# First-stage tiles take the gates' first loads, the first tokens' weight splits leave GpSimd, and the base tiles' transfers move to SyncE's queue

## The chip, the cores and the metric

The kernel runs on one core of a Trainium2 chip. The metric is the device time of one execution in microseconds (us), lower is better. Engines are named as the profile names them: PE (TensorE), DVE (VectorE), ACT (ScalarE), POOL (GpSimd) and SP (SyncE, which here only issues transfers). POOL and ACT can issue transfers too; each engine works through its own instructions in program order, so a transfer that waits holds what stands behind it on that engine.

## The reference, cut to what matters

One encoder layer over 2048 tokens and 16 learned meta tokens, D = 1024, all in float32:

```python
h = layer_norm(concat([meta, x]), ln_in_g, ln_in_b)
q, k, v, u, g_attn, g_ssm = split(h @ w_in[l], SPLITS)
q = rope(rms_norm(q, q_norm_g)); k = rope(rms_norm(k, k_norm_g))
y_attn = block_attention(q, k, v)
y_ssm  = s5_branch(u, ...)                  # forward and backward scan, GELU-GLU
merged = sigmoid(g_attn) * (y_attn @ w_attn_br) + sigmoid(g_ssm) * (y_ssm @ w_ssm_br)
h = layer_norm(ALPHA * h + merged @ w_o, ln1_g, ln1_b)
moe = expert_choice_moe(h[real tokens])     # 16 experts, each takes its top 256 tokens, SwiGLU
h = layer_norm(ALPHA * h + moe, ln2_g, ln2_b)
return h[real tokens]
```

## The kernel before, in words

Products that must keep float32 are made of a high and a low part: ACT casts a weight `wr` to `wh`, DVE (or POOL) subtracts to get `wl`, and PE adds three products (high by high, high by low, low by high). Every engine's order is the order of the Python code.

**First stage** (`phase_a`). Seventeen token tiles of 128 tokens (the last holds the 16 meta tokens) are normalised (`ln_ops`, `norm`), turned by PE (`trans`: PE writes `pT`, ACT casts `hth`, DVE subtracts `htl`), and multiplied with the q/k/v columns (`qkv`, the first weights, split by `split_w(0, k)`) and the u columns (`u_mm`, the second weights, `split_w(1, k)`, which run three raw tiles deep). `rope` finishes q and k of a tile on DVE with the products `gc` and `gs` that POOL makes in `rope_prep`. `qk_trans` turns q and k with PE, casts to `qh` on ACT, subtracts to `ql` on DVE, and stores them to `q_d` and `k_d`: through SP's queue, for the last three tiles through POOL's. Each `qh` buffer is used again two tiles later, after its store has landed. A loop over s runs the stages of five neighbouring tiles side by side.

**Gates** (`gates`). A generator, started at step s = 17 of that loop, loads raw weights (512 KB each), splits them to `gwh` and `gwl`, loads the normalised, turned inputs back from `ht_d` (256 KB for each of k = 0..7 and of high and low, for four token blocks b), multiplies (`pg`, line 1230), and takes the sigmoid on ACT (`gg`, line 1201). The state-space part's first loads on ACT (lines 708 and 710) stand ahead of the first `gg`.

**Attention, merge, routing** follow and are not touched.

**Experts** (`experts`). Each of the 16 experts has 12 weights of 1 MB. An expert is 16 steps: 8 gate/up steps of 48 matmuls (gate block i and up block i are both used in steps 2i and 2i+1), then 8 down steps of 24. `ahead` in a step loads the weight three further on through SP's queue and splits the one two further on (ACT `wh`, DVE `wl`); three raw buffers let SP run ahead of the steps. The output rows are added into `acc_d` by indirect transfers of POOL, two halves per expert (`scatter`; the second half is issued in step 1 of the next expert). From expert 9 on `step` also advances side generators once per step. `finish` takes the base tiles: all 16 tiles of 128 rows of `acc_d` are read (`fx`), normalised in pairs (`norm`, ACT sums into `fj`, DVE the rest, one new pair every 11 steps) and stored to the output. `redo` does the rows that experts 9 to 14 changed again (`fa`), and the last expert normalises its own rows (`ye`) half by half. `fx` loads and stores go through POOL's queue, as `scatter`, the gathers `xg` and the indirect stores (`put_rows`) do:

```python
            def load(t):
                xs[t] = fp.tile([128, D], F32, name="fx", bufs=4)
                PL.dma_start(xs[t], acc_d[128 * t:128 * t + 128])
```

Of the kernel before, what the change touches and what calls it, by code (L numbers as in the profile page):

```python
# [10 lines left out]
F32 = mybir.dt.float32  # L11
# [33 lines left out]
def f(t):  # L45
    return t.bitcast(F32)
# [3 lines left out]
def kernel(ctx, tc, x, meta, ln_in_g, ln_in_b, w_in, q_norm_g, k_norm_g,  # L50
# [63 lines left out]
        for _ in ln_ops(*args):  # L114
            pass

    def phase_a(start_gates):
        cr = ExitStack()
        with ExitStack() as c:
            wq = cr.enter_context(pool(name="a_q", bufs=1, side="right"))  # L120
            xp = cr.enter_context(pool(name="a_x", bufs=4, side="right"))
            px = cr.enter_context(pool(name="a_px", bufs=1, space=PSUM, side="right"))
            wp = c.enter_context(pool(name="a_w", bufs=1))
            sm = c.enter_context(pool(name="a_sm", bufs=3))
# [11 lines left out]
                SP.dma_start(RC[t][0], rope_c[128 * t:128 * t + 128])  # L136
                SP.dma_start(RC[t][1], rope_s[128 * t:128 * t + 128])

            gb = wq.tile([128, D], F32, name="gb")
            bb = wq.tile([128, D], F32, name="bb")  # L140
            cols = ((0, 768), (768, 1280))
            WH, WL, WR = [], [], []
            for p, (c0, c1) in zip((wq, wp), cols):
# [18 lines left out]

            def rope_prep(t):
                cs, sn = RC[t]
                gc, gs = (xp.tile([128, 10, 64], F32, name="gc", bufs=2), xp.tile([128, 10, 64], F32, name="gs", bufs=2))
                PL.tensor_tensor(gc, g10, cs[:, None, :].to_broadcast([128, 10, 64]), op=OP.mult)
                PL.tensor_tensor(gs, s10, sn[:, None, :].to_broadcast([128, 10, 64]), op=OP.mult)
                RC[t] = gc, gs
# [123 lines left out]
            with pool(name="a_st", bufs=8) as st:  # L292
                for k in range(8):
                    load_w(st, 0, k)
                load(2)
                for _ in zip(*(ln_ops(sm, X[t], 128, gb, bb, "a") for t in range(2))):
                    pass
                for k in range(3):
                    split_w(0, k, PL)
                trans(0)  # L300
                trans(1)
                qkv(0, 0, 2)
                qkv(1, 0, 2)
                for k in range(2, 8):
                    if k > 2:
                        split_w(0, k, V)
                    qkv(0, k, k + 1)
                    qkv(1, k, k + 1)
# [12 lines left out]
                load_w(wr, 1, k)  # L321
            load(3)
            norm(2)
            for k in range(8):
                split_w(1, k, (V, PL)[k % 2])
                if k + 3 < 8:
                    load_w(wr, 1, k + 3)
                if k == 4:
                    load_rope(2)
                    load_rope(3)  # L330
# [4 lines left out]
            for s in range(NT + 4):  # L335
                if s + 4 <= NT:
                    load(s + 4)
                    if s + 4 < NT:
                        load_rope(s + 4)
                if s < NT:  # L340
                    rope_prep(s)
                if 1 <= s < NT:
                    trans(s + 1)
                if 0 <= s - 3 < NT:
                    qk_trans(s - 3, 0)
                next(gg, None)
                if 1 < s <= NT:
                    qkv(s, 0, 3)
                next(gg, None)
                if 0 <= s - 3 <= NT:  # L350
                    qk_trans(s - 3, 1)
                next(gg, None)
                if 2 < s + 2 <= NT:
                    norm(s + 2)
                if 0 <= s - 1 <= NT:
                    rope(s - 1)
                if 1 < s <= NT:
                    qkv(s, 3, 8)
                if 1 <= s <= NT:
                    u_mm((s - 1) // 2, (s - 1) % 2)  # L360
                if s == NT:
                    cr.close()
                    gg = start_gates()
                    next(gg)
                    u_meta()
        return gg
# [792 lines left out]

        yield from pipe((item(b) for b in range(4)), every=7)  # L1160

    def gates(c):
        hp = c.enter_context(pool(name="g_h", bufs=32, side="right"))
        wp = c.enter_context(pool(name="g_w", bufs=2, side="right"))
        pg = c.enter_context(pool(name="g_p", bufs=2, space=PSUM, side="right"))
        W, HB = {}, {}
        order = [(i, b) for i in range(2, 16) for b in range(2)]
        order += [(16, 2), (17, 2), (16, 3), (17, 3)] + [(i, b) for i in range(18, 32) for b in (2, 3)]
        steps = [[(0, 0), (1, 0)], [(0, 1), (1, 1)]] + [[x] for x in order]
        first = {}  # L1170
        for s, group in enumerate(steps):
            for i, b in group:
                first.setdefault(i, s)
        split_at = {first[i] if i != 17 else first[i] + 2: i + 1 for i in range(2, 31)}
        load_at = {first[i]: i + 2 for i in range(2, 30)}

        def load_w(i):
            c0 = 1280 + 128 * (i % 16)
            wr = wp.tile([128, 8, 128], F32, name="gwr")
            SP.dma_start(wr, w_in[0, :, c0:c0 + 128].rearrange("(k p) c -> p k c", p=128))  # L1180
            W[i] = wr

        def split_w(i):
            wr = W[i]
            wh = wp.tile([128, 8, 128], F32R, name="gwh")
            wl = wp.tile([128, 8, 128], F32R, name="gwl")
            A.copy(wh, wr)
            V.tensor_tensor(wl, wr, f(wh), op=OP.subtract)
            W[i] = wh, wl

        def load_h(b, k):
            r = []
            for i in range(2):
                t = hp.tile([128, 512], F32R, name="gh")
                SP.dma_start(f(t), ht_d[i, k, :, 512 * b:512 * b + 512])
                r.append(t)
            HB[b, k] = r

        def evac(i, b, p):
            g = wp.tile([128, 512], F32, name="gg")  # L1200
            A.activation(g, p, AF.Sigmoid)  # L1201
            A.dma_start(gt_d[i % 16, :, 512 * b:512 * b + 512], g)

        load_w(0)
        load_w(1)
        for k in range(8):
            load_h(0, k)
        yield
        split_w(0)
        split_w(1)  # L1210
        load_w(2)
        load_w(3)
        for k in range(8):
            load_h(1, k)
        ev = []
        for step, group in enumerate(steps):
            while len(ev) + len(group) > 2:
                evac(*ev.pop(0))
            if step in split_at:
                split_w(split_at[step])  # L1220
            if step in load_at:
                load_w(load_at[step])
            P = [pg.tile([128, 512], F32, name="pg") for _ in group]
            n = 0
            for k in range(8):
                for (i, b), p in zip(group, P):
                    wh, wl = W[i]
                    hi, lo = HB[b, k]
                    for j, (w, h) in enumerate(((wh, hi), (wh, lo), (wl, hi))):
                        PE.matmul(p, w[:, k], h, start=(k == 0 and j == 0), stop=(k == 7 and j == 2))  # L1230
                        n += 1
                        if n % 4 == 0:
                            if n == 12 and ev:
                                evac(*ev.pop(0))
                            yield
                if group[0][0] == 15:
                    load_h(b + 2, k)
            ev = [(i, b, p) for (i, b), p in zip(group, P)]
            if step == 1:
                split_w(2)  # L1240
        for e in ev:
            evac(*e)
# [428 lines left out]
    def experts(c, pos, inf):  # L1671
# [221 lines left out]
        def finish():  # L1893
            SP.dma_start(gb, row_bcast(ln2_g, D))
            SP.dma_start(bb, row_bcast(ln2_b, D))
            xs = {}

            def load(t):
                xs[t] = fp.tile([128, D], F32, name="fx", bufs=4)
                PL.dma_start(xs[t], acc_d[128 * t:128 * t + 128])  # L1900

            yield
            for t in range(2):
                load(t)
            yield
            yield

            def base(t):
                for n, _ in enumerate(norm([xs[t], xs[t + 1]])):
                    if n == 7 and t + 2 < NT:  # L1910
                        load(t + 2)
                        load(t + 3)
                    yield
                for i in range(2):
                    PL.dma_start(outs[t + i], xs.pop(t + i))

            yield from pipe((base(t) for t in range(0, NT, 2)), every=MO[3])

# [12 lines left out]
        def step(e, s):  # L1931
# [4 lines left out]
            if (e, s) == (E - 1, 1):  # L1936
                acc_rows(e)
                sides.append(redo(e - 1, MO[2]))
            for g in sides:
                next(g, None)  # L1940

        one_hot(0, 0, NT)
        pi = pick(0)
# [79 lines left out]
                pass  # L2023
        return
    cg = ExitStack()
    gg = phase_a(lambda: gates(cg))
    if stop <= 1:
        return
    with cg:
# [101 lines left out]
```

## Time and profile before

| | |
|---|---|
| three timed runs | 3157.53, 3164.89, 3165.57 us (median 3164.89) |
| the profiled execution's own time | 3158.51 us |
| its span in the trace | 3156.7 us |
| PE busy | 2978.7 us (94% of the span) |
| DVE, ACT, POOL busy | 2145.9, 1572.0, 1010.9 us |
| mean granted clock of PE | 0.977 of full speed |

The span is from the first to the last recorded instruction. All times of the trace below are counted from its start. A share of busy time is an average over stages that have different limits, so a stage is read from its own rows.

### The profile page before, as it was taken

Reading aid. Unit: us, or ns where it says so; the run is one execution under the profiler, and the core shown is the slowest. Engines: PE = TensorE matmul, PEld = TensorE weight load, DVE = VectorE, ACT = ScalarE, POOL = GpSimd, SP = SyncE. Lnnn points to the kernel's source line nnn. Section 1 sums busy time; section 2 is a strip of 40 time slices with the busy share of each in tenths; the row PEclk is TensorE's granted clock in tenths of the full one; section 3 lists DMA queues with packets and bytes.
Section 4 is the critical chain, followed back from the end, with each engine's and each line's share of the span. In section 5 each row is a group of like instructions: output and inputs, shape, how many; then the busy total and the mean of one; then the engine's idle time right before and its main releaser. Section 6 shows DMA issues by size and latency. Waiting matters only on the chain.

```text
span 3156.7 us, 56179 instructions
## 1 busy us (share of the span) xinstructions
PE 2978.7 (94%) x22829; PEld 2632.0 (83%) x22829; DVE 2145.9 (68%) x3725; ACT 1572.0 (50%) x2229; POOL 1010.9 (32%) x633
## 2 busy tenths in 40 slices
PE   6999999999989999999899996799999999999997
PEld 5887787777867777777678885699999999999997
DVE  7886589783366666666466666666666665778886
ACT  2222352243369999999622222344444444666553
POOL 3221035051069999999510001111111101122221
PEclk9999999999999999999999998799999999999999
DMA  6566633557510101013366743366677667778884
GB/s 224 186 206 186 160 104 108 185 148 203 175 45 22 35 21 35 21 35 90 110 206 199 200 134 108 134 214 206 214 220 225 217 214 230 258 260 267 274 263 157
DMA packets 464499, 513.00 MB, mean 163 GB/s; under 512 B 47568, under 2 KB 387728, under 8 KB 463856
## 3 DMA queue, kind: packets, MB, share of 16 engines
q1 hardware_dynamic: 433616, 421.20, 42.7%
q0 software_dynamic: 19232, 69.53, 7.3%
q10 hardware_dynamic: 11392, 18.68, 1.7%
q8 instruction: 179, 2.93, 0.4%
q14 instruction: 80, 0.66, 0.1%
HBM read 385.59 MB, written 123.76 MB: 161 GB/s over the span
## 4 chain that ended last, share of the span: by engine, by line
PE 62%; DVE 14%; ACT 8%; DMA 6%; issue 6%; POOL 3%; SPq 1%; ACTq 0%; POOLq 0%; DVEq 0%
PE pg L1784 18%; PE pd L1812 8%; PE pg L1230 7%; PE pw L1383 5%; PE pb L1315 5%; PE pm L449 3%; PE pS L483 3%; ACT pe L490 2%; PE pS L484 2%; PE po L520 2%; DVE wl L1692 2%; PE pz L1147 1%; ACT wh L1691 1%; POOL pl L506 1%; ACT ph L502 1%
## 5 line engine op out<-in xcount | busy, mean ns | idle before, releaser
L1784 PE MATMUL pg<-xh,wh 128*128 128x256 f32 x2048 | 573.0, 280 | 5.5 <-DVE sg L1792 4.6
L1784 PE MATMUL pg<-xh,wl 128*128 128x256 f32 x2048 | 570.3, 278 | 2.8 <-DVE wl L1692 2.8
L1692 DVE TENSOR_TENSOR wl<-wr,wh 128x2048 fp32r<-128x2048 f32 x189 | 433.2, 2292 | 204.2 <-ACT wh L1691 204.1
L1784 PE MATMUL pg<-xl,wh 128*128 128x256 f32 x2048 | 570.6, 279 | 0.0
L506 POOL TENSOR_TENSOR pl<-pe,ph 128x1024 f16<-128x1024 f32 x256 | 542.5, 2148 | 60.5 <-DVE ph L500 48.8
L455 DVE TENSOR_REDUCE mx<-pm 128x1 f32<-128x412 f32 (+1 forms) x640 | 368.6, 586 | 190.1 <-PE pm L449 174.1
L1784 PEld LDWEIGHTS pg<-xh,wh 128*128 128x128 f32 x2048 | 386.6, 189 | 6.3 <-DVE sg L1792 4.8
L1784 PEld LDWEIGHTS pg<-xh,wl 128*128 128x128 f32 x2048 | 385.8, 188 | 3.5 <-DVE wl L1692 3.4
L1784 PEld LDWEIGHTS pg<-xl,wh 128*128 128x128 f32 x2048 | 386.3, 189 | 0.0
L1691 ACT CAST wh<-wr 128x2048 fp32r<-128x2048 f32 x189 | 359.8, 1904 | 16.3 <-DMA wr<-in_w_up_e_dram 9.2
L1230 PE MATMUL pg<-gh,gwh 128*128 128x512 f32 x1024 | 337.0, 405 | 19.5 <-ACT gg L1201 14.1
L490 ACT ACTIVATE pe<-pS,ebias 128x1024 f32<-128x1024 f32 x256 | 284.8, 1112 | 37.9 <-PE pS L484 37.9
L1812 PE MATMUL pd<-wh,hh 128*128 128x256 f32 x1024 | 285.8, 279 | 7.0 <-ACT ye L1831 4.6
L1812 PE MATMUL pd<-wh,hl 128*128 128x256 f32 x1024 | 283.7, 277 | 1.5 <-DVE hl L1799 1.4
L1812 PE MATMUL pd<-wl,hh 128*128 128x256 f32 x1024 | 283.1, 276 | 0.0
L1230 PEld LDWEIGHTS pg<-gh,gwh 128*128 128x128 f32 x1024 | 195.4, 194 | 62.7 <-ACT gg L1201 16.8
L502 ACT CAST ph<-pe 128x1024 f16<-128x1024 f32 x224 | 234.4, 1046 | 16.1 <-ACT pe L490 0.4
L449 PE MATMUL pm<-k,q 128*128 128x412 f32 (+1 forms) x640 | 233.5, 375 | 9.1 <-DVE mx L455 3.1
L483 PE MATMUL pS<-q,k 128*128 128x512 f32 (+1 forms) x544 | 231.8, 426 | 10.6 <-ACT pe L490 9.2
L520 PEld LDWEIGHTS <-ph 128*128 128x128 f16 (+1 forms) x2176 | 188.7, 96 | 63.6 <-issue 60.3
L520 PE MATMUL po<-v,ph 128*128 128x129 f16 (+1 forms) x2176 | 231.5, 221 | 0.8 <-ACT t L528 0.8
L522 PE MATMUL po<-v,pl 128*128 128x65 f16 (+1 forms) x2176 | 220.2, 192 | 2.2 <-POOL pl L506 2.1
(424 smaller groups left out, 6761.5 us busy)
## 6 DMA issues: line engine op xcount, KB each, us to landing
wr<-in_w_gate_e_dram SPq DMA_DIRECT2D x64, 1024.0 KB
wr<-in_w_up_e_dram SPq DMA_DIRECT2D x64, 1024.0 KB
wr<-in_w_down_e_dram SPq DMA_DIRECT2D x64, 1024.0 KB
gwr<-in_w_in_dram SPq DMA_DIRECT2D x32, 512.0 KB
gh<-ht_d SPq DMA_DIRECT2D x64, 256.0 KB
gt_d<-gg ACTq DMA_DIRECT2D x64, 256.0 KB
gt<-gt_d SPq DMA_DIRECT2D x32, 512.0 KB
q<-q_d SPq DMA_DIRECT2D x96, 128.0 KB
```

Source lines behind the costliest of these rows:

```text
L449: PE.matmul(p[:, :w], Q[n][0][:, 128 * j:128 * j + 128], K1[units[n][1] // 4][:, k0:k0 + w], start=True, stop=True)
L455: V.tensor_reduce(MX[n][:, j, c:c + 1], p[:, :w], axis=AX.X, op=OP.max)
L483: PE.matmul(p[:m, a], K2[g][:, k0:k0 + m], Q[n][1], start=True, stop=False)
L490: A.activation(e[:m, :w], p[:m, :w], AF.Exp, bias=ebias[:m], scale=HD ** -0.5)
L502: A.copy(hi[:m, :w], e[:m, :w])
L506: (PL if w == 2 else V).tensor_tensor(lo[:m, :w], e[:m, :w], hi[:m, :w], op=OP.subtract)
L520: PE.matmul(o[:, 0:129], hi[:m, a, 128 * j:128 * j + 128], v16[:m, kt, g, 0:129], start=(kt == 0 and j % 2 == 0), stop=False, skip_group_c ...
L1230: PE.matmul(p, w[:, k], h, start=(k == 0 and j == 0), stop=(k == 7 and j == 2))
L1691: A.copy(wh, wr)
L1692: V.tensor_tensor(wl, wr, f(wh), op=OP.subtract)
L1784: PE.matmul(p[:, gu], w[:, k, cs_], x[:, k], start=(k == 0 and j == 0), stop=(k == 7 and j == 2))
L1812: PE.matmul(p, a[:, k, cs_], w[:, k], start=(k == 0 and j == 0), stop=(k == 7 and j == 2))
```

## The change

There are four edits. (1) In `phase_a` the first three weight splits of the q/k/v columns run on DVE between the turns of the first two tiles, no longer on POOL; and the normalisation of tile 3 runs two operations at a time between the splits of the second weights instead of after them. (2) The pool of the first stage's token tiles stays open. The gates' raw weights go into the two tiles that held the layer norm's gain and bias (`bb`, `gb`), and the inputs k = 0..3 of token blocks 0 and 2 into the four token tiles `x`, so that those ten loads don't wait for the stage's other pools to close; they are issued at s = 17 ahead of the stores of tile 14. The two first gate splits stand ahead of the meta tokens' u. (3) The base tiles' loads and stores go through SP's queue, and their normalisation begins four steps after the first load instead of two. (4) In the last expert from step 10 on the side generators advance twice a step.

```diff
+        xp = cg.enter_context(pool(name="a_x", bufs=4, side="right"))
...
-                for k in range(3):
-                    split_w(0, k, PL)
+                split_w(0, 0, V)
                 trans(0)
+                split_w(0, 1, V)
                 trans(1)
+                split_w(0, 2, V)
...
+            ln3 = ln_ops(sm, X[3], 128, gb, bb, "a")
             for k in range(8):
                 split_w(1, k, (V, PL)[k % 2])
+                if k > 1:
+                    next(ln3, None)
+                    next(ln3, None)
...
+                if s == NT:
+                    gg = start_gates(xp)
+                    next(gg)
                 if 0 <= s - 3 < NT:
                     qk_trans(s - 3, 0)
...
-                if 2 < s + 2 <= NT:
+                if 3 < s + 2 <= NT:
                     norm(s + 2)
...
+        def load_x(b, k):
+            t = xp.tile([128, 2, 512], F32R, name="x")
+            for i in range(2):
+                SP.dma_start(f(t[:, i]), ht_d[i, k, :, 512 * b:512 * b + 512])
+            HB[b, k] = [t[:, 0], t[:, 1]]
...
+        load_w(0)
+        load_w(1)
+        for k in range(NX):
+            load_x(0, k)
+        yield
+        hp = c.enter_context(pool(name="g_h", bufs=32 - 2 * NX, side="right"))
...
-                PL.dma_start(xs[t], acc_d[128 * t:128 * t + 128])
+                SP.dma_start(xs[t], acc_d[128 * t:128 * t + 128])
...
-            yield
-            yield
+            for _ in range(4):
+                yield
...
-                    PL.dma_start(outs[t + i], xs.pop(t + i))
+                    SP.dma_start(outs[t + i], xs.pop(t + i))
...
-            for g in sides:
-                next(g, None)
+            for _ in range(2 if (e, s) >= (E - 1, 10) else 1):
+                for g in sides:
+                    next(g, None)
```

How the instructions stand on the engines at three places. First DVE at the start, from the first two tiles' last normalising operation (L107 x2) to the splits of the first weights; line numbers of the changed kernel are one higher here. Before:

```order
L106 SCALAR_TENSOR_TENSOR x<-x,amv,gb 128x1024 x2
L107 SCALAR_TENSOR_TENSOR x<-x,ar,bb 128x1024 x2
L184 TENSOR_TENSOR htl<-pT,hth 128x4x128 x4
L157 TENSOR_TENSOR wl<-wr,wh 128x768 x5
L103 BN_STATS ast<-x 128x6 x2
```

and of the change:

```order
L106 SCALAR_TENSOR_TENSOR x<-x,amv,gb 128x1024 x2
L107 SCALAR_TENSOR_TENSOR x<-x,ar,bb 128x1024 x2
L158 TENSOR_TENSOR wl<-wr,wh 128x768
L185 TENSOR_TENSOR htl<-pT,hth 128x4x128 x2
L158 TENSOR_TENSOR wl<-wr,wh 128x768
L185 TENSOR_TENSOR htl<-pT,hth 128x4x128 x2
L158 TENSOR_TENSOR wl<-wr,wh 128x768 x6
L103 BN_STATS ast<-x 128x6 x2
```

DVE has eight splits instead of five; POOL's first tensor operations are now the second weights' (L158, 128x512), behind two copies that wait for the q and k gains.

Second, SP's queue at the end of the first stage, from the last u store of the main loop (`u_d`) over the stores of tile 14 (`q_d`, `k_d`, `v_d`) to the gates' loads. Before:

```order
L273 DMA u_d<-us 8x16x128 x4
L256 DMA q_d<-qh 128x4x128
L256 DMA q_d<-ql 128x4x128
L258 DMA k_d<-qh 128x128
L258 DMA k_d<-ql 128x128
L213 DMA v_d<-vt 128x128
L1180 DMA gwr<-in_w_in_dram 128x8x128 x2
L1195 DMA gh<-ht_d 128x512 x16
L1180 DMA gwr<-in_w_in_dram 128x8x128 x2
```

and of the change:

```order
L274 DMA u_d<-us 8x16x128 x4
L1188 DMA bb<-in_w_in_dram 128x8x128
L1188 DMA gb<-in_w_in_dram 128x8x128
L1180 DMA x<-ht_d 128x512 x8
L257 DMA q_d<-qh 128x4x128
L257 DMA q_d<-ql 128x4x128
L259 DMA k_d<-qh 128x128
L259 DMA k_d<-ql 128x128
L214 DMA v_d<-vt 128x128
L1224 DMA gh<-ht_d 128x512 x8
L1188 DMA bb<-in_w_in_dram 128x8x128
```

Ten loads (3 MB) have moved ahead of the five stores, and eight loads are left behind them.

Third, SP's queue in expert 9, from the loads of `finish`'s gain and bias (`gb_`, `bb_`) on; `wr` are the experts' weights in order, the gate block behind `bb_` is expert 9's weight 4. Before:

```order
L1895 DMA bb_22041<-in_ln_b_dram 128x1024
L1684 DMA wr<-in_w_gate_e_dram 128x8x256
L1684 DMA wr<-in_w_up_e_dram 128x8x256
L1684 DMA wr<-in_w_gate_e_dram 128x8x256
L1684 DMA wr<-in_w_up_e_dram 128x8x256
L1684 DMA wr<-in_w_down_e_dram 128x8x256 x4
```

and of the change:

```order
L1922 DMA bb_22037<-in_ln_b_dram 128x1024
L1711 DMA wr<-in_w_gate_e_dram 128x8x256
L1927 DMA fx<-acc_d 128x1024 x2
L1711 DMA wr<-in_w_up_e_dram 128x8x256
L1711 DMA wr<-in_w_gate_e_dram 128x8x256
L1711 DMA wr<-in_w_up_e_dram 128x8x256
L1711 DMA wr<-in_w_down_e_dram 128x8x256 x4
L1711 DMA wr<-in_w_gate_e_dram 128x8x256
L1711 DMA wr<-in_w_up_e_dram 128x8x256
L1927 DMA fx<-acc_d 128x1024 x2
L1711 DMA wr<-in_w_gate_e_dram 128x8x256
L1942 DMA out_dram<-fx 128x1024 x2
```

The first two `fx` loads stand between weights 4 and 5. The eight pairs of loads fall into steps 1 and 12 of expert 9, 7 of 10, 2 and 13 of 11, 8 of 12, 3 and 14 of 13; the eight pairs of stores into steps 14 of expert 9, 9 of 10, 4 and 15 of 11, 10 of 12, 5 of 13, 0 and 11 of 14.

## Rows read from the trace of the kernel before

**Rows 1.** The page's chain of work that ended last, shares by engine.

```profile
PE 62%; DVE 14%; ACT 8%; DMA 6%; issue 6%; POOL 3%; SPq 1%; ACTq 0%; POOLq 0%; DVEq 0%
```

**Rows 2.** Windows, experts 8, 9, 15: length, busy (PE, PEld, DVE, ACT, POOL), clock, DMA.

```profile
2561.92:2630.10 68.18, 68.18 (x627) 68.14 (x625) 43.46 (x64) 32.94 (x40) 7.79 (x5) 1.00 0.73 225
2630.10:2706.23 76.13, 71.50 (x626) 71.07 (x625) 49.97 (x83) 39.48 (x52) 9.43 (x11) 0.96 0.74 241
...
3069.26:3137.73 68.47, 66.20 (x578) 65.64 (x576) 48.99 (x76) 30.43 (x38) 14.61 (x9) 1.00 0.61 193
```

**Rows 3.** Timeline of DVE, start: start, length, what, [idle before <-releaser].

```profile
12.15 5.57 DVE L107 SCALAR_TENSOR_TENSOR x<-x,ar,bb 128x1024 f32<-128x1024 f32 x2
...
53.65 1.28 DVE L107 SCALAR_TENSOR_TENSOR x<-x,ar,bb 128x1024 f32<-128x1024 f32 x1
```

**Rows 4.** Timeline of POOL, the same stretch.

```profile
11.37 8.03 POOL L157 TENSOR_TENSOR wl<-wr,wh 128x768 fp32r<-128x768 f32 x3 [10.92 <-ACT wh L156]
...
45.94 1.56 POOL L166 TENSOR_TENSOR gc<-g,cs 128x640 f32<-128x640 f32 x1
```

**Rows 5.** Timeline of PE, 54 to 60 us.

```profile
55.09 1.94 PE L176 MATMUL pT<-idf,x 128*128 128x128 f32 x8 [4.30 <-DVE x L107]
58.75 0.77 PE L203 MATMUL pq<-wh,hth 128*128 128x512 f32 x1 [1.73 <-DVE sq L232]
```

**Rows 6.** Timeline of SP's queue, start of the gates.

```profile
286.91 0.40 SPq L256 DMA_DIRECT2D q_d<-qh  x1
...
290.90 13.93 SPq L1195 DMA_DIRECT2D gh<-ht_d  x16
```

**Rows 7.** Timeline of ACT, start of the gates.

```profile
300.28 0.57 ACT L251 CAST qh<-pk 128x512 fp32r<-128x512 f32 x1
...
309.42 0.59 ACT L251 CAST qh<-pk 128x512 fp32r<-128x512 f32 x1 [1.89 <-DMA q_d<-qh]
...
317.21 0.17 ACT L251 CAST qh<-pk 128x16 fp32r<-128x16 f32 x1 [4.29 <-DMA q_d<-qh]
...
319.91 1.81 ACTq L708 DMA_DIRECT2D s<-in_ssm_a_im_dram  x2
322.73 0.37 ACTq L710 DMA_DIRECT2D s<-in_ssm_log_dt_dram  x1
...
324.42 0.60 ACT L1201 ACTIVATE gg<-pg 128x512 f32<-128x512 f32 x1
```

**Rows 8.** Timeline of PE, 324 to 326 us.

```profile
325.07 1.22 PE L1230 MATMUL pg<-gh,gwh 128*128 128x512 f32 x2 [6.49 <-ACT gg L1201]
```

**Rows 9.** Timeline of SP's queue: expert 9's weight 5, expert 13's weight 7.

```profile
2634.93 0.38 SPq L1684 DMA_DIRECT2D wr<-in_w_up_e_dram  x1
...
2944.16 0.37 SPq L1684 DMA_DIRECT2D wr<-in_w_up_e_dram  x1
```

**Rows 10.** Timeline of POOL, experts 9 and 13.

```profile
2642.71 1.62 POOL L1834 DMA_INDIRECT acc_d<-ye,ix  x1 [0.30 <-ACT sg L1790]
2652.59 2.23 POOL L1900 DMA_DIRECT2D fx<-acc_d  x4 [8.26 <-DMA acc_d<-ye,ix]
...
2954.64 1.16 POOL L1900 DMA_DIRECT2D fx<-acc_d  x2 [9.01 <-DMA acc_d<-ye,ix]
```

**Rows 11.** Timeline of ACT, experts 9 and 13.

```profile
2659.00 1.06 ACT L1874 ACTIVATE fj<-fx 128x1024 f32<-128x1024 f32 x1 [8.93 <-DMA fx<-acc_d]
...
2955.05 1.92 ACT L1691 CAST wh<-wr 128x2048 fp32r<-128x2048 f32 x1 [0.39 <-DMA wr<-in_w_up_e_dram]
```

**Rows 12.** Timeline of DVE, the last expert's second half of rows.

```profile
3140.55 0.48 DVE L1818 SCALAR_TENSOR_TENSOR ye<-pd,gv,ye 128x256 f32<-128x256 f32 x1
...
3144.31 1.28 DVE L1827 SCALAR_TENSOR_TENSOR ye<-ye,lr,bb 128x1024 f32<-128x1024 f32 x1
```

**Rows 13.** Timeline of POOL, the last two stores.

```profile
3144.50 1.91 POOL L1890 DMA_INDIRECT out_dram<-ye,io  x1 [2.62 <-DMA out_dram<-fa,io]
3149.54 0.95 POOL L1890 DMA_INDIRECT out_dram<-ye,io  x1 [3.12 <-DMA out_dram<-ye,io]
```

More of the change, by code (lines that the diff above doesn't have):

```diff
@@ L115, in layer_norm, with phase_a @@
             pass
-    def phase_a(start_gates):
+    def phase_a(cg, start_gates):
         cr = ExitStack()
+        xp = cg.enter_context(pool(name="a_x", bufs=4, side="right"))
         with ExitStack() as c:
             wq = cr.enter_context(pool(name="a_q", bufs=1, side="right"))
-            xp = cr.enter_context(pool(name="a_x", bufs=4, side="right"))
+            xg = cr.enter_context(pool(name="a_g", bufs=2, side="right"))
             px = cr.enter_context(pool(name="a_px", bufs=1, space=PSUM, side="right"))
@@ L137, in load_rope @@
                 SP.dma_start(RC[t][1], rope_s[128 * t:128 * t + 128])
-            gb = wq.tile([128, D], F32, name="gb")
-            bb = wq.tile([128, D], F32, name="bb")
+            gb = xp.tile([128, D], F32, name="gb", bufs=1)
+            bb = xp.tile([128, D], F32, name="bb", bufs=1)
             cols = ((0, 768), (768, 1280))
@@ L164, in rope_prep @@
                 cs, sn = RC[t]
-                gc, gs = (xp.tile([128, 10, 64], F32, name="gc", bufs=2), xp.tile([128, 10, 64], F32, name="gs", bufs=2))
+                gc, gs = (xg.tile([128, 10, 64], F32, name="gc"), xg.tile([128, 10, 64], F32, name="gs"))
                 PL.tensor_tensor(gc, g10, cs[:, None, :].to_broadcast([128, 10, 64]), op=OP.mult)
@@ L343, in phase_a @@
                     trans(s + 1)
+                if s == NT:
+                    gg = start_gates(xp)
+                    next(gg)
                 if 0 <= s - 3 < NT:
                     qk_trans(s - 3, 0)
-                next(gg, None)
+                if s > NT:
+                    next(gg, None)
                 if 1 < s <= NT:
                     qkv(s, 0, 3)
-                next(gg, None)
+                if s > NT:
+                    next(gg, None)
                 if 0 <= s - 3 <= NT:
                     qk_trans(s - 3, 1)
-                next(gg, None)
-                if 2 < s + 2 <= NT:
+                if s > NT:
+                    next(gg, None)
+                if 3 < s + 2 <= NT:
                     norm(s + 2)
@@ L362, in phase_a @@
                     cr.close()
-                    gg = start_gates()
                     next(gg)
@@ L1160, in glu, with gates, load_w @@
         yield from pipe((item(b) for b in range(4)), every=7)
-    def gates(c):
-        hp = c.enter_context(pool(name="g_h", bufs=32, side="right"))
+    def gates(c, xp):
+        HB = {}
+        NX = 4
+        def load_x(b, k):
[3 more added lines that the diff above has]
+            HB[b, k] = [t[:, 0], t[:, 1]]
+        W = {}
+        def load_w(i):
+            c0 = 1280 + 128 * (i % 16)
+            wr = xp.tile([128, 8, 128], F32, name="gb" if i % 2 else "bb", bufs=1)
+            SP.dma_start(wr, w_in[0, :, c0:c0 + 128].rearrange("(k p) c -> p k c", p=128))
+            W[i] = wr
+        load_w(0)
[4 more added lines that the diff above has]
+        hp = c.enter_context(pool(name="g_h", bufs=32 - 2 * NX, side="right"))
         wp = c.enter_context(pool(name="g_w", bufs=2, side="right"))
         pg = c.enter_context(pool(name="g_p", bufs=2, space=PSUM, side="right"))
-        W, HB = {}, {}
         order = [(i, b) for i in range(2, 16) for b in range(2)]
@@ L1175, in gates @@
         load_at = {first[i]: i + 2 for i in range(2, 30)}
[L1177 to L1181, printed above, removed]
         def split_w(i):
@@ L1191, in load_h @@
         def load_h(b, k):
+            if b % 2 == 0 and k < NX:
+                load_x(b, k)
+                return
             r = []
@@ L1202, in evac @@
             A.dma_start(gt_d[i % 16, :, 512 * b:512 * b + 512], g)
-        load_w(0)
-        load_w(1)
-        for k in range(8):
+        for k in range(NX, 8):
             load_h(0, k)
-        yield
         split_w(0)
         split_w(1)
+        yield
         load_w(2)
@@ L1904, in finish @@
                 load(t)
-            yield
-            yield
+            for _ in range(4):
+                yield
             def base(t):
@@ L2025 @@
     cg = ExitStack()
-    gg = phase_a(lambda: gates(cg))
+    gg = phase_a(cg, lambda xp: gates(cg, xp))
     if stop <= 1:
```

## The prediction

> **What bounds the kernel now.** I read the chain of waits first: 62% of it is PE, 14% DVE, 8% ACT, 6% transfers [rows 1]. PE is the limit nearly everywhere, so the change can win only where PE stands still or where the end of the program hangs on another engine. I then cut the expert stage into windows by the first matmul of each expert. Expert 8, which has no side work, takes 68.18 us with PE busy throughout; expert 9 takes 76.13 with PE idle for 4.63 and the clock at 0.96; from expert 9's start at 2630.10 to the last matmul's end at 3137.73 pass 507.6 us, 30.4 more than seven times 68.18 [rows 2]. That is all that edits (3) and (4) could win ahead of the last matmul. Last I read the timelines of each engine at the four places that the diff touches: the start, the start of the gates, experts 9 to 13, and the tail behind 3137.73.
>
> **Edit 1, the first tokens.** POOL's three splits run from 11.37 to 19.40, and beside them DVE's two L107 take 5.57 us, where one takes 1.28 alone [rows 3, 4]. Without POOL the two take some 2.6; the first tile is ready about 1.5 us earlier, the second 3. DVE gets three splits more, of at most 2.7 us each (POOL's price, 8.03 for three [rows 4]), in gaps in which it waits for ACT's cast of the turned tile; PE's first products hide them. Tile 3's normalisation no longer stands between the last split and `rope` on DVE. In the trace PE waits 4.30 us for it at 55.09, and 1.73 at 58.75 for the `rope` work queued behind it [rows 5]. Together 6.0 us, and behind this place PE is the bound until the gates, so they would stay won. Against it: POOL's first tensor operation is now the second weights' split. Before the old first one POOL stood still for 10.92 us from the span's start [rows 4]; whatever it costs to make a tensor operation ready lay hidden in there, so it is between nothing and 10.9. The nearest row is `gc`, also a kind of work that POOL had not done before, which took 1.56 us at once [rows 4]. At nothing the edit wins 6; at 10.9 POOL's `gc` at 45.94 moves behind 55, and nothing is won. I take 5, because a few us of delay fit before tile 3's products are due.
>
> The Trainium skill bears on that cost: its page "GPSIMD Engine Reference", section "Instruction dispatch", says that the first call of a freshly loaded kernel pays some 6 us that no row of a profile shows. No row here can show it; by that figure, an estimate, the edit would win about 4 instead of 5.
>
> **Edit 2, the gates' start.** SP issues the `q_d` store of tile 14 at 286.91 and 16 input loads in 13.93 us, 0.87 each [rows 6]. Ten loads ahead of the store push it by 8.7 us to 295.6. The next `qh` cast, now at 300.28, uses that store's buffer again. Stores of this stretch land late: `qh` cast at 300.28 (0.57 us) is stored by POOL, and the cast that needs its buffer starts at 309.42, 8.6 us later [rows 7]. With 8.6 the moved store lands at 304.2 and the cast is 4 us late; with half of that it is not late. What follows hangs on it: two rounds of cast and store (300.28, 309.42, 317.21), the state-space loads to 322.73, and `gg` at 324.42 [rows 7], for which PE waits 6.49 us at 325.07 [rows 8]. So the gates' first product may well start earlier, since its data are there sooner, but it only lengthens that wait. For the change speaks that the issue at L710 starts 1.0 us after the one before it is done (319.91 and 1.81 against 322.73 [rows 7]), and that 3 MB less stand in the queues when POOL's two stores pass. I take 0 (from -4, half of both rounds' excess, to +4).
>
> **Edit 3, the base tiles on SP's queue.** This is the largest term. The first pair of `fx` must wait until expert 8's second half has been added into `acc_d`: POOL issues that at 2642.71, and the `fx` behind it goes out at 2652.59, when it has landed [rows 10]. On POOL only POOL waited. On SP the weights wait: weight 5 of expert 9 went out at 2634.93 [rows 9], and now goes out behind two `fx` (0.56 each, a quarter of 2.23) at 2653.7. How long it takes to land lies between 6.4 (the first `fx`, 2652.59 to 2659.00 [rows 10, 11]) and 10.9 (a weight of expert 13, 2944.16 to 2955.05 [rows 9, 11]); with four transfers at once I take 8: 2661.7. Cast on ACT takes 1.9 [rows 11], DVE's half about the same: 2665.5. PE wants weight 5 in the middle of step 4; a step of 48 matmuls is a twelfth of 68.18, 5.68 us, so at 2630.10 + 4.5 x 5.68 = 2655.7. PE stands for 9.8 us. The stall of before goes: ACT waited 8.93 us for `fx` at 2659.00 [rows 11] and PE 4.63; two steps more of lead put this sum behind the landing. Net +5. In expert 13 the pair in step 3 waits in the same way, until 2954.64 [rows 10]; weight 7, issued at 2944.16 [rows 9], goes out at 2955.8 and is there at 2963.8 instead of 2955.05. A weight is cast in the step for which 8.5 us are left (1.5 steps), 3.8 of them needed for the split, so 4.7 of the 8.8 are hidden, less what ACT and DVE lose: +5 with the clock that a stall costs (0.96 in expert 9 [rows 2]). Expert 11's pair, in step 2, holds weight 6, which is cast two steps ahead (7.6 hidden): +3. The eight pairs of stores hold SP until DVE has done a tile in the same step, while SP otherwise runs some two steps ahead; two down steps are 5.7 us, 4.7 of which are hidden: up to 1 each, I take 3 in all. POOL is freed of 32 transfers and their waits, so its scatters and gathers go out when they can: -4 (bounds 0 and, by the 8.93 alone, -9). Sum +12. The ends: if weights come in time after all, expert 9's 8 us vanish and ACT's waits too, -13; if each of the three late weights takes 10.9 instead of 8 and POOL's relief is nothing, +25.
>
> **Edit 4, the tail.** PE ends at 3137.73 [rows 2], but DVE takes up the last quarter of the second half's rows only at 3140.55, behind the redone rows, and ends the normalisation at 3145.59 [rows 12], 5.04 us later. POOL issues the store of the first half at 3144.50, after the redone rows' store has landed, and the second at 3149.54, when the first has landed, 5.04 later [rows 13]. With the side work done earlier DVE starts at 3137.8 and ends at 3142.9; the first half's store goes out at about 3137.8 and is landed by 3142.9 too. The last store then goes out 6.6 earlier. I take -6 (at least -2.8, DVE's part alone).
>
> **Sum.** -5 + 0 + 12 - 6 = +1, on the profiled execution's own 3158.51 (the span of 3156.7 and 1.8 around it): 3159.5. The median of the timed runs is 6.4 above the profiled execution, one of the three runs 1 below it; I add half of 6.4: **3163 us**. A difference under 0.3%, 9.5 us, can hardly be told from no change here.
>
> **The rivals.** *Weights in time (faster).* SP runs far enough ahead, or the transfers land sooner from SP's queue than from POOL's, and edit 3 only takes expert 9's stall away: -5 to -13 for it, sum about -19, 3143. For it: 30.4 us of excess in experts 9 to 15, which POOL's late `fx` began [rows 2, 11]; against it, the order in which weight 5 stands behind a transfer that cannot go before 2652. Beside it stands a rule of the Trainium skill, "SBUF — State Buffer", the warning on the "DVE blocks DMA" trap: transfers issued by GpSimd can wait for their descriptors while DVE holds the shared port, those of SP's queue don't. By it the `fx` on SP would land sooner than 6.4. No row separates the two.
>
> *SP's queue held (slower).* The pairs of `fx` and stores in SP's order delay weights by more than the lead at each of experts 9, 11 and 13: +25 for edit 3, sum +14, 3176. It decides from a landing time of about 10 us behind `fx`; expert 13's 10.9 speaks for it, the 6.4 against.
>
> *POOL's first operation is dear (no change).* Edit 1 wins nothing: sum +6, 3168.
>
> **Chances.** My forecast, with the third rival beside it, has 0.41 (within 0.3%); weights in time and a full win at the start and the tail 0.35 (faster); SP held 0.24 (slower). The range 3145 to 3179 takes in most of both sides; the forecast's own is 3154 to 3172.
>
> **What would show it.** Right: in PE's timeline no wait for L107 near 55 and the first long `pq` block some 5 us earlier; `gg` within 3 us of the same distance from the first stage's end; PE standing still in the middle of expert 9's step 4, waiting for DVE's `wl`, with weight 5 issued just after the scatter's landing; expert 13's weight 7 likewise; the span's end 12 to 13 us behind PE's end instead of 19 (3156.7 against 3137.73). Wrong: expert 9 as short as expert 8, POOL's first split later than 40, or ACT's `qh` cast past 304.

## The result and the profile after

The changed kernel takes 3194.35 us (median of 4 runs, 3189.82 to 3196.71), before 3163.55: a ratio of 1.0099, 95% interval 1.0081 to 1.0117. It is 31 us slower, where I had forecast no change (3163, range 3145 to 3179). The profiled execution took 3196.71, with a span of 3194.9, 38.2 more than before; that is more than 31 because it is the slowest of the four, and the one profiled before was among the faster.

Where the 38.2 us came in is read from where the same matmul stands in both traces. The last `pu` matmul of the first stage ends at 296.78 instead of 299.76 (-3.0). At the first matmul of expert 9, 2630.41 against 2630.10 [rows 2], nothing of this is left (+0.3; in the twelve later profiles this point lay between 2623.7 and 2630.7, also for edits that don't touch the stages between, so a few us there can't be assigned). Experts 9 to 15 take 553.8 us instead of 507.6 (+46.2). From PE's last matmul to the span's end pass 10.7 us instead of 19.0 (-8.3). The windows of the changed kernel, cut as in [rows 2] (expert 9, 12, 15, and the stretch behind PE's end):

```profile
2630.41:2709.03 78.62, 71.60 (x627) 71.08 (x625) 49.03 (x81) 37.49 (x48) 7.80 (x5) 0.93 0.68 214
...
2862.28:2950.25 87.97, 73.95 (x627) 72.64 (x625) 61.51 (x107) 43.69 (x60) 13.65 (x8) 0.92 0.70 227
...
3111.43:3184.20 72.77, 68.79 (x578) 67.73 (x576) 54.06 (x79) 31.35 (x40) 15.81 (x10) 1.00 0.64 208
...
3184.20:3194.90 10.70, 0.00 (x0) 0.00 (x0) 4.96 (x13) 0.29 (x1) 1.90 (x2) 0.64 0.25 98
```

Before, expert 12 and experts 9 to 15 together were:

```profile
2850.99:2925.91 74.92, 70.47 (x626) 69.83 (x625) 62.02 (x109) 45.05 (x62) 17.12 (x13) 1.00 0.80 266
2630.10:3137.73 507.63, 488.69 (x4322) 483.30 (x4320) 389.75 (x683) 286.72 (x382) 104.44 (x83) 0.99 0.78 253
```

Every one of the seven experts is longer, by 2.5, 2.0, 6.5, 13.0, 11.3, 6.6 and 4.3 us; expert 12 most, 88.0 instead of 74.9. Busy times of DVE and ACT over the seven have hardly changed (392.0 and 286.2 us), and the DMA share of expert 12 has fallen from 0.80 to 0.70. So it is waiting, not work. What SP's queue waited for between 2636 and 3195 us (view of waits: engine and what it wanted to issue, what released it, us in total, times, longest), the largest lines on `fx`:

```profile
SPq L1927 <- DMA acc_d<-ye,ix: 48.5, 6, 14.1
SPq L1942 <- DMA out_dram<-fa,io: 43.3, 2, 25.2
...
SPq L1942 <- DVE fx L1914: 32.1, 4, 10.0
SPq L1942 <- DVE sg L1818: 27.6, 3, 9.7
```

L1927 are the `fx` loads, L1942 the stores. The longest single wait of these, 25.2 us, is a store that waits for an indirect store of redone rows (`fa`) into the same output to land. In SP's timeline of that stretch it stands between two weights of expert 12:

```profile
2852.07 0.38 SPq L1711 DMA_DIRECT2D wr<-in_w_gate_e_dram  x1
2877.75 1.16 SPq L1942 DMA_DIRECT2D out_dram<-fx  x2
2879.00 1.69 SPq L1711 DMA_DIRECT2D wr<-in_w_up_e_dram  x1
```

POOL issues that indirect store only at 2869.76, after 60.48 us in which it waited for DVE; ACT and PE pay, in their timelines:

```profile
2869.76 5.56 POOL L1917 DMA_INDIRECT out_dram<-fa,io  x1 [60.48 <-DVE oh L1750]
```

```profile
2887.88 1.90 ACT L1718 CAST wh<-wr 128x2048 fp32r<-128x2048 f32 x1 [17.84 <-DMA wr<-in_w_up_e_dram]
```

```profile
2889.83 0.58 PE L1811 MATMUL pg<-xh,wh 128*128 128x256 f32 x1 [10.16 <-ACT wh L1718]
```

The store waits, the weight behind it goes out 27 us after the one ahead of it, ACT waits 17.84 us for that weight, PE 10.16 us for ACT. The `fx` loads do the same in expert 11: SP stands from 2790.32 until 2806.83, when a scatter has landed, ACT waits 11.78 us for the weight behind, and PE waits for work that ACT and DVE had to leave standing:

```profile
2806.83 0.81 SPq L1927 DMA_DIRECT2D fx<-acc_d  x2
2808.04 0.38 SPq L1711 DMA_DIRECT2D wr<-in_w_gate_e_dram  x1
```

```profile
2817.70 1.90 ACT L1718 CAST wh<-wr 128x2048 fp32r<-128x2048 f32 x1 [11.78 <-DMA wr<-in_w_gate_e_dram]
```

```profile
2824.39 0.55 PE L1811 MATMUL pg<-xh,wh 128*128 128x256 f32 x1 [7.64 <-DVE sg L1819]
```

The three other stages, each with a row of the changed kernel: PE at the start (beside [rows 5]), POOL's first tensor operation (beside [rows 4]), the first gate on ACT (beside [rows 7]), and the last store (beside [rows 13]):

```profile
56.08 0.47 PE L204 MATMUL pq<-wh,hth 128*128 128x512 f32 x1 [3.51 <-DVE sq L233]
```

```profile
32.53 1.29 POOL L158 TENSOR_TENSOR wl<-wr,wh 128x512 fp32r<-128x512 f32 x1 [1.48 <-ACT wh L157]
```

```profile
308.70 0.58 ACT L252 CAST qh<-pk 128x512 fp32r<-128x512 f32 x1 [5.88 <-DMA q_d<-qh]
...
322.52 0.60 ACT L1230 ACTIVATE gg<-pg 128x512 f32<-128x512 f32 x1
```

```profile
3189.93 0.95 POOL L1917 DMA_INDIRECT out_dram<-ye,io  x1 [4.53 <-DVE ye L1854]
```

### The profile page after: what moved, and what is told of

Same layout as the page of the kernel before. It is cut to its first block, busy times and chain, and to the rows that moved or that the text cites. A ratio compares the mean times of both kernels' runs of the same rounds, so it can differ in the third digit from the quotient of the medians.

```text
span 3194.9 us, 56196 instructions
## 1 busy us (share of the span) xinstructions
PE 2992.8 (94%) x22829; PEld 2644.5 (83%) x22829; DVE 2146.2 (67%) x3728; ACT 1571.1 (49%) x2229; POOL 986.1 (31%) x598
## 4 chain that ended last, share of the span: by engine, by line
PE 57%; DVE 14%; DMA 9%; ACT 8%; issue 7%; POOL 3%; SPq 1%; ACTq 0%; POOLq 0%; DVEq 0%
PE pg L1811 17%; PE pd L1839 7%; PE pg L1257 6%; PE pw L1410 5%; PE pb L1342 5%; PE pm L460 3%; PE pS L494 3%; ACT pe L501 2%; PE pS L495 2%; PE po L531 2%; PE pz L1158 1%; DVE wl L1719 1%; DMA wr<-in_w_up_e_dram 1%; ACT wh L1718 1%; POOL pl L517 1%
## 5 line engine op out<-in xcount | busy, mean ns | idle before, releaser
L1811 PE MATMUL pg<-xh,wh 128*128 128x256 f32 x2048 | 579.4, 283 | 32.6 <-ACT wh L1718 18.0
L1257 PE MATMUL pg<-gh,gwh 128*128 128x512 f32 x768 | 252.5, 405 | 8.6 <-DMA gh<-ht_d 5.6
L1861 POOL DMA_INDIRECT acc_d<-ye,ix x30 | 65.4, 2181 | 528.1 <-ACT ye L1858 517.0
```

What stands on the lines that cost most here:

```text
L1811: PE.matmul(p[:, gu], w[:, k, cs_], x[:, k], start=(k == 0 and j == 0), stop=(k == 7 and j == 2))
```

## The experiments

Theory M: SP's queue is held. A transfer that waits on SP stops all that stands behind it, and what stands behind it are the weights. Rival R: it is the bytes; 16 MB more in the weights' queue make every weight land later, whenever they are issued. Rival Q: the side work of DVE and ACT has moved (four steps, double steps) and the queue has nothing to do with it. All times are medians; the ratio is to the kernel before, timed on the same chip. "Experts" below is the length of experts 9 to 15 in the profile. One profile shows one execution: two later kernels that leave the expert stage as it was before (`only_1` and `only_2`) take 511.4 and 515.4 us there instead of 507.6, so a difference of up to 8 us between two profiles need not be an effect of the edit.

**Stores back on POOL, loads on SP** (`stores_pool`).

```diff
-                    SP.dma_start(outs[t + i], xs.pop(t + i))
+                    PL.dma_start(outs[t + i], xs.pop(t + i))
```

> The changed kernel with the base tiles' 16 stores back on POOL's queue; the 16 fx loads stay on SP's. Theory M (SP is held: each store waits on SP for DVE's last operation on its tile, and for the landing of an earlier indirect store into the output, and the weights stand behind it): the stores' share of the loss, about 28 of the 46 us in experts 9 to 15, goes; expert 12, now 88.0 us, falls below 78; time about 3166. Rival R (it is the transfers themselves: 16 MB more in the weights' queue make every weight land later, whenever they are issued): half of the transfers are gone, so about half of the loss, 3171 to 3175, and it goes evenly from all experts. Rival Q (the loss is from side work that moved on DVE and ACT, four yields and the double steps): 3190 to 3195.

3183.64 us, ratio 1.0051 (1.0035 to 1.0068); experts 542.1:

```profile
2628.10:3170.20 542.10, 499.77 (x4322) 493.73 (x4320) 392.71 (x685) 285.86 (x382) 98.42 (x68) 0.96 0.74 238
```

Q's range is missed, and so are the other two. M's number was too good by 18 us: the loads alone cost far more than I had thought, and expert 12 still takes 83.0, not under 78 (it takes 79.2 even with nothing on SP, in the run after the next).

**Loads back on POOL, stores on SP** (`loads_pool`).

```diff
-                SP.dma_start(xs[t], acc_d[128 * t:128 * t + 128])
+                PL.dma_start(xs[t], acc_d[128 * t:128 * t + 128])
```

> The changed kernel with the base tiles' 16 fx loads back on POOL's queue; the stores stay on SP's. Theory M: the weights no longer wait for scatters to land; experts 9, 11 and 13 lose their late weight 5, 6 and 7 (stalls of 7.0, 7.6 and 4.0 us in PE), expert 12 keeps its 10 us stall; about 12 to 16 us faster than the changed kernel, about 3180. Rival R: half of the loss, 3171 to 3175, from all experts alike. Rival Q: 3190 to 3195.

3179.58 us, ratio 1.0044 (1.0028 to 1.0061), as M had it; experts 536.7. Expert 9 takes 68.2 instead of 78.6, expert 12 keeps 86.8 with a wait of 10.85 us on PE. Expert 13 falls by 4.3, about as M had it, but expert 11 only by 1.9, not by 7.6.

**Both back on POOL** (`both_pool`): both diffs above.

> The changed kernel with loads and stores of the base tiles on POOL's queue, four steps between first load and first normalisation, the double steps and the rest kept. Theories M and R: the whole loss goes, experts 9 to 14 take 430 to 440 us together as before (439) or less, since expert 9's stall for the first fx goes too; the span still ends about 11 us behind PE's end instead of 19; about 3150 to 3157, faster than the kernel before. Rival Q: 3190 to 3195.

3149.03 us, ratio 0.9945 (0.9929 to 0.9962): 45 us below the changed kernel (49 by the ratios) and faster than the kernel before. Q falls: the four steps and the double steps are still in. What is won over the kernel before does not lie in experts 9 to 15 (509.8 instead of 507.6) but in the stretch behind PE's end (12.9 instead of 19.0) and ahead of expert 9 (4.9, which is within the scatter at that point). The windows for expert 9, expert 12 and experts 9 to 15:

```profile
2625.19:2693.37 68.18, 68.18 (x626) 68.14 (x625) 49.21 (x81) 37.33 (x48) 8.82 (x9) 1.00 0.82 262
2834.44:2913.59 79.15, 73.25 (x627) 72.04 (x625) 63.48 (x109) 46.33 (x64) 17.98 (x14) 0.98 0.78 258
2625.19:3134.96 509.77, 490.24 (x4322) 485.52 (x4320) 393.28 (x685) 285.50 (x382) 112.12 (x85) 0.99 0.78 253
```

Against these 509.8 the loads on SP alone cost 32.3, the stores alone 26.9, both together 44.0. The two don't add up; I take it that a weight that is late already isn't late twice, which no run tests by itself.

**Stores four steps later, on SP** (`stores_later`).

```diff
+                for _ in range(4):
+                    yield
                 for i in range(2):
                     SP.dma_start(outs[t + i], xs.pop(t + i))
```

> The changed kernel with the stores of each pair of base tiles four steps later in the program, still on SP's queue, with the same bytes. Theory M: DVE is done with the tile when SP comes to the store, so the waits on SP for DVE's operations (some 90 us in all, of which part is hidden) go; where an earlier indirect store has to land first the wait stays if that store is issued late; 15 to 28 us faster than the changed kernel, 3166 to 3179. Rival R: the transfers are the same, so 3190 to 3197. Rival Q: the same, 3190 to 3197.

3190.93 us, ratio 1.0077 (1.0060 to 1.0094): within R's range, outside M's. The waits for DVE are gone from SP's largest waits, but those for indirect stores to land are four instead of two, 34.2 us, the longest 18.0. That one has moved into expert 15, which takes 85.2 (at a granted clock of 0.90):

```profile
SPq L1927 <- DMA acc_d<-ye,ix: 51.7, 6, 13.4
SPq L1944 <- DMA out_dram<-fa,io: 34.2, 4, 18.0
```

```profile
3092.75:3177.96 85.21, 72.13 (x578) 71.08 (x576) 52.41 (x79) 30.74 (x38) 15.46 (x11) 0.90 0.57 186
```

So this run doesn't decide between M and R: the wait was moved, not taken away. The next three do.

**The wait without the bytes: stores** (`tiny_stores`), on top of both on POOL:

```diff
+                    SP.dma_start(outs[t + i][0:1, 0:16], xs[t + i][0:1, 0:16])
                     PL.dma_start(outs[t + i], xs.pop(t + i))
```

> Base tiles' loads and stores on POOL's queue as in the run with both there (3149 us), and beside each store one of 64 bytes (the same values, of the tile's first row) on SP's queue at the stores' place: SP waits for the same things as with the full stores, but moves next to no bytes. Theory M (SP is held by the wait): experts 9 to 15 take about 537 us as with the full stores on SP, time 3173 to 3181. Rival R (the bytes in the weights' queue): 510 us as with both on POOL, 3147 to 3153.

3175.98 us, ratio 1.0034 (1.0019 to 1.0048); experts 534.9, beside 536.7 with the full stores:

```profile
2625.45:3160.39 534.94, 498.18 (x4322) 492.05 (x4320) 392.18 (x685) 286.80 (x382) 107.66 (x85) 0.97 0.74 241
```

```profile
SPq L1942 <- DVE fx L1914: 60.6, 9, 10.3
SPq L1942 <- DMA out_dram<-fa,io: 43.3, 2, 25.3
```

Sixteen transfers of 64 bytes cost nearly as much as sixteen of 512 KB, with the same 25 us wait for the indirect store. Their bytes without the wait were not run for the stores.

**The wait without the bytes: loads** (`tiny_loads`):

```diff
                 PL.dma_start(xs[t], acc_d[128 * t:128 * t + 128])
+                SP.dma_start(fp.tile([1, 16], F32, name="fy", bufs=4), acc_d[128 * t:128 * t + 1, 0:16])
```

> The same with one load of 64 bytes of acc_d on SP's queue beside each fx load of POOL: SP waits for the scatters' landing as with the full loads and moves next to no bytes. Theory M: experts 9, 11 and 13 get their late weights 5, 6 and 7 back, 535 to 542 us for experts 9 to 15, time 3174 to 3184. Rival R: 510 us, 3147 to 3153.

3181.44 us, ratio 1.0054 (1.0035 to 1.0073), beside 3183.64 and 1.0051 with the full loads: the same. The experts take 535.9, beside 542.1 with the full loads and 509.8 with none, but this profile is of the fastest of the four executions (3173.92).

**The bytes without the wait** (`free_bytes`):

```diff
+                SP.dma_start(xs[t], h1_d[128 * t:128 * t + 128])
                 PL.dma_start(xs[t], acc_d[128 * t:128 * t + 128])
```

> The same without the small transfers, but SP's queue loads 512 KB of rows of another tensor, long written, into each fx tile at the loads' place before POOL's own load (8 MB more in the weights' queue, with no wait for scatters; those rows are overwritten by the right ones). Theory M: SP is held at most until the tile's earlier store has landed, so nearly no loss, 3149 to 3158. Rival R: the weights behind land later at eight places, 3165 to 3180.

3158.24 us, ratio 0.9977 (0.9967 to 0.9987), 9 us more than without the loads; experts 515.1, 5.3 more than without:

```profile
2629.54:3144.65 515.11, 493.00 (x4322) 488.26 (x4320) 393.03 (x685) 286.20 (x382) 108.70 (x85) 0.98 0.81 267
```

8 MB more in the same queue at the same places cost 5 us in the profile, 9 by the medians, where the wait alone cost 26 in the profile and 32 by the medians. R falls as the main cause. What is left of it is small and not well known: expert 11 alone takes 75.4 instead of 69.5 in this profile, but 74.3 in the next run too, where no bytes are added and nothing ahead of the last expert is changed.

**Without the double steps** (`both_pool_no4`): both on POOL, edit 4 undone.

```diff
-            for _ in range(2 if (e, s) >= (E - 1, 10) else 1):
-                for g in sides:
-                    next(g, None)
+            for g in sides:
+                next(g, None)
```

> Both on POOL's queue, without the double steps in the last expert (edit 4 undone). If the double steps give the short tail (12.9 us behind PE's end instead of 19.0) and cost the last expert's longer stretch (71.8 us instead of 68.5), the last expert falls to 68 to 69 and the tail grows to about 19: 3 us slower than with them, about 3152. If the tail is short because the side work starts two steps differently, the tail stays at 13 and the time falls to about 3146.

3157.57 us, ratio 0.9972 (0.9960 to 0.9983). The tail is 18.7 us (12.9 with the double steps), expert 15 takes 69.7 (71.8 with them). The double steps give 5.8 behind PE's end and cost 2.1 ahead of it; the ratios 0.9945 and 0.9972 say rather more, 8 us, with intervals that just overlap. Some 5 us of that stand in expert 11 of this profile (74.3 instead of 69.5), which the edit does not touch, so the net 3.7 is the better reading.

**Single edits on the kernel before**: edit 1 alone (`only_1`), edit 2 alone (`only_2`), the four steps alone (`only_yields`), and the fast version without edit 2 (`both_pool_no2`). Their diffs are the parts of the change's diff; `only_yields` is this:

```diff
-            yield
-            yield
+            for _ in range(4):
+                yield
```

> The kernel before with edit 1 alone (first splits on DVE, tile 3's normalisation between the second weights' splits). In the trace of the full change the first stage ends 3.0 us earlier and POOL's first split shows no delay: if that is edit 1's, the first stage ends 3 us earlier here too and, as nothing behind it is changed, the time falls by 3, a ratio of 0.999. If the 3 us need edit 2's pools, nothing moves.

3160.89 us, ratio 0.9991 (0.9981 to 1.0000). The last `pu` matmul ends 2.1 us earlier; at the edge of what can be told.

> The kernel before with edit 2 alone (gates' first loads into the first stage's tiles, ahead of tile 14's stores). My prediction's step: the moved store delays the cast of tile 14's q and what follows, against the earlier loads: 0 plus or minus 4 us. In the trace of the full change the first gate came 1.9 us earlier while the first stage ended 3.0 earlier, so about +1: 3163 to 3167. The rival, that the earlier first products are a gain: -3 to -5.

3158.57 us, ratio 0.9982 (0.9973 to 0.9991): some 5 us faster, outside the 3163 to 3167 that I had and nearer the rival's 3 to 5. In the profile the last `pu` ends 0.2 later, `gg` starts at 324.50 beside 324.42, and expert 9 begins at 2630.66 beside 2630.10. But the profiled execution took 3166.78, the slowest of the eleven, so it can't show where the median's 5 us come from. Left open.

> The kernel before with only the start of the base tiles' normalisation moved from two to four steps behind the first loads, loads and stores on POOL's queue. If expert 9's 8 us over the others (76.1 instead of 68.2) are ACT waiting for fx ahead of a weight's cast, expert 9 falls to 68.2 and the time by up to 8, about 3157; the later experts may take some of it back, since the base tiles end two steps later. If they are not, nothing moves.

3157.86 us, ratio 0.9988 (0.9978 to 0.9998). The time is the 3157 that I had, but by luck. Expert 9 falls from 76.1 to 68.2, as expected; experts 12 to 14 take back most of it (79.3, 74.9 and 75.4 instead of 74.9, 70.5 and 72.9), so experts 9 to 15 are 508.9 instead of 507.6, and the profile does not show where the median's gain lies.

```profile
2628.00:2696.20 68.20, 68.20 (x627) 68.16 (x626) 49.24 (x81) 37.35 (x48) 8.81 (x9) 1.00 0.81 263
```

> Edits 1 and 4 and the four steps, base tiles on POOL's queue, the gates' start as before. If edit 2 is worth nothing by itself, as the prediction had it, this is as fast as the run with edit 2 and both on POOL's queue: 3147 to 3153. If edit 2 is part of that run's gain, 3153 to 3157.

3149.09 us, ratio 0.9962 (0.9949 to 0.9974), the same median as with edit 2 (3149.03), but timed on another chip; by the ratios, 0.9962 and 0.9945, edit 2 is worth between nothing and some 5 us, as in `only_2`. The best version is therefore the change without the moves to SP's queue; whether edit 2 adds to it stays open.

## Why the prediction was wrong

**The step that failed is edit 3's term, +12 with ends of -13 and +25; experts 9 to 14, where it acts, took 41.9 us more in the change's own trace, and experts 9 to 15 took 44.0 more than in the same kernel with both on POOL.** The mechanism was the second rival's, SP's queue held; the forecast had the same mechanism, at too small a size. The term was mis-sized by a factor of three and a half, and no run shows its one negative part, POOL's relief.

*The stores* were priced at up to 1 us a pair, 3 in all, because I let each wait only for DVE's operation two steps away and set the weight's lead against it. Alone they cost 26.9 us. Two things were missing. First, SP waited up to 10 us for DVE, not 5.7. Second, a store into the output also waits for the indirect stores of redone rows into the same output to have landed, and those stand behind POOL's own waits. The prediction did not name this wait. Two such waits, of 25.2 and 18.0 us, end in experts 12 and 14, which grew by 13.0 and 6.6 us and to which the prediction gave nothing of their own; the first explains expert 12's 10.16 us on PE. How the 26.9 us divide between the two kinds of waits was not tested.

*The loads* were priced at 5, 3 and 5 for experts 9, 11 and 13. The three places were right: in the change's trace SP waited for scatters there and nowhere else, some 21, 16 and 11 us (the view counts six waits, since each place has two). Expert 9 was read well: weight 5 went out at 2652.20 (2653.7 in the prediction), ACT began its cast at 2659.50 (2661.7), and PE stood from 2655.96 to 2663.78 but for two matmuls, 7.0 us of waiting where I had 9.8:

```profile
2661.45 0.58 PE L1811 MATMUL pg<-xh,wh 128*128 128x256 f32 x1 [5.49 <-ACT wh L1718]
2663.78 0.58 PE L1811 MATMUL pg<-xh,wl 128*128 128x256 f32 x1 [1.53 <-DVE wl L1719]
```

Against the kernel before this expert is 2.5 us longer, where I had 5. Expert 11 is the miss. With the loads alone on SP it takes 84.0 us, 14.5 more than with both on POOL and 9.9 more than before, where I had 3 (the number is rough, since this expert takes 69.5 to 79.2 us in runs in which SP is not held). Expert 12 took 3.8 more, where I had nothing. And the stall of before that I set against expert 9's wait was no gain for the stage: in `only_yields`, where the four steps remove it, experts 12 to 14 take it back.

*POOL's relief*, -4, is not to be seen: with POOL freed, its indirect stores still waited for DVE (the 60.48 us above). Counted from the expert's first matmul, the gathers `xg` go out 9.3 us earlier in expert 11, but 0.8 to 5.2 later in experts 12 to 14. No run prices it alone.

**Edit 1, -5**: the mechanism holds, the size was -3.0 in the change's trace (-2.1 alone). Tile 3's normalisation no longer stops PE, and L107's pair takes 2.47 instead of 5.57, but PE waits 3.51 us before 56.08 for the `rope` work; I had counted all waiting there as gone. The third rival, that POOL's first tensor operation is dear, falls: it started 1.48 us after the copies, when ACT's cast was done, and took 1.29, as later ones do. The figure of 6 us from the Trainium skill's "GPSIMD Engine Reference" (section "Instruction dispatch") is not seen in this case.

**Edit 2, 0**: the store was issued at 295.47, as worked out (295.6), and `gg` came 1.9 us earlier where the stage ended 3.0 earlier. That is +1 in the trace, within the range; the timed runs of `only_2` say -5, outside it, and this stays open.

**Edit 4, -6**: -8.3 behind PE's end, but +4.3 in expert 15 (72.8 instead of 68.5), whose `down` products wait for DVE. I had left out that work done earlier is done beside something: -4 net in the change's trace, -3.7 in the pair of profiles without the move to SP (5.8 less 2.1). So some of the -8.3 seems to be edit 3's, since without it the double steps shorten the tail by 5.8.

## What to carry to other kernels

Before a transfer moves to another engine's queue, list everything it waits for, ordering against other writers of the same tensor included, and look up when each of them is done; then look at what stands behind it on the new queue. A queue that runs ahead of the compute is worth its lead only while nothing in it waits, and here transfers of 64 bytes that waited cost nearly as much there as transfers of 512 KB. When a change has several edits, price each against the kernel with the others, since one may already remove the stall that another is credited for.

## What the runs showed of the hardware

The bytes themselves were cheap: 8 MB more through the weights' queue raised the DMA share of experts 9 to 15 from 0.78 to 0.81 and cost 5.3 us of 510 in the profile, 9 us by the medians.

And a stall of PE costs more than its length. In expert 9 of the changed kernel, behind the two waits of 5.49 and 1.53 us, the granted clock stood at 0.50, the lower of its two levels (1.2 GHz), and was full again from 2670 on:

```profile
2663.78:2667.00 3.22, 3.22 (x15) 3.22 (x16) 3.19 (x5) 1.03 (x2) 0.00 (x0) 0.50 0.88 276
2670.00:2673.00 3.00, 3.00 (x27) 3.00 (x27) 2.08 (x2) 2.97 (x5) 0.00 (x0) 1.00 0.50 173
```

So PE was busy for 71.60 us in this expert, where the same expert with both on POOL needs 68.18 at a clock of 1.00: 7.0 us of waiting and 3.4 us of slower matmuls make up the 10.4 that it lost.
